# An encoder layer on one core: the merge gates in seven-product pairs, on inputs normalised in place

## The chip, the core and the metric

The kernel runs on one NeuronCore of a Trainium2 chip. The metric is device time in microseconds, from several executions; one further execution is recorded by the hardware profiler. Engines are named as in the profile: PE is TensorE (PEld its weight loads), DVE is VectorE, ACT is ScalarE, POOL is GpSimd, SP is SyncE, which issues most of the DMAs.

## What is computed

One pre-norm residual layer over 256 tokens of width 2048, then a final RMSNorm. Everything is float32. Cut to what matters:

```
h    = rms_norm(x, norm_g)                              # (256, 2048)
proj = h @ w_in                                         # q k v o za | gif | xb zb | ga gb
ya   = mlstm(q, k, v, gif) * sigmoid(o) * silu(za)      # bidirectional, 4 heads of 512
yb   = rglru(xb) * silu(zb)                             # bidirectional recurrence, 2048 channels
merged = sigmoid(ga) * (ya @ w_branch_a) + sigmoid(gb) * (yb @ w_branch_b)
out  = rms_norm(x + merged @ w_out, final_g)
```

The work is matrix products of a 256 x 2048 input with weights of 2048 columns each: GA and GB are the two merge gates' products with h, and wa, wb, wo stand for w_branch_a, w_branch_b and w_out.

## The kernel before

**Products in three parts.** Each float32 operand is split in two float32r parts, hi and lo, and a product is the sum of three matmuls: hi·hi, hi·lo and lo·hi. A weight chunk (128 x 1024, 512 KB, for two of the 16 k-tiles of 128 and 512 output columns) is loaded by SP into one of five `raw` buffers; ScalarE casts it to `whi` (L123), VectorE subtracts to get `wlo` (L124). There are four buffers of each, so that a cast waits until TensorE has used the chunk four before it. `load_chunk` is that helper. A block is 512 output columns; it takes eight chunks (kq = 0 to 7) and has its sums in one `acc` tile (two of PSUM's eight banks, two such tiles). The other four banks are `aux` 0 to 3.

**Three forms of block.** `block_nat` gives a block with tokens on the partitions: per chunk 2 k-tiles x 2 token blocks x 3 = 12 matmuls of 512 columns (L138 to L140). `half_tr` gives the transposed form. `pair` takes two neighbouring blocks at once, and for the chunks in a given list it computes the 4 x 4 block products of two k-tiles, two token blocks and two column blocks with seven products in place of eight (a Winograd form). p1, p5, p7, p6 collect the common products, `banks` the rest. For such a chunk pair VectorE and ScalarE make sums of the weights (`t1`, `t2`) and split three of them, h1, h2, h3, and one half `b` (lines L157 and L158, buffers `b11`, `whi`, `wlo`), and `make_form` makes the sums of the inputs beforehand. Other chunks of a pair are plain, as in `block_nat`. After the last seven-product chunk the p's are combined into the result (L220 to L224), and after the last chunk the banks are added (L231).

**The order of the work.** q and k blocks, then four times a block of xb (`rg_block`) and a head (`head`: blocks V, O, Z and the head's output), then four zb blocks, the wb pairs, GB, GA and wa pairs interleaved, and wo: block 2, a pair of blocks 0 and 1, block 3 last. `h` is stored as hi and lo of x times norm_g, without the inverse root of the mean square, in the tile `sHL` (`hhi`, `hlo`); the factor per token is applied later, as `rstd` where tokens are on the partitions (a scale in the eviction), as the row `rbc` where they are on the free axis (a multiplication by VectorE). Small pieces of work (norms, gates, scores, the transposes `fin` and `fin_m`) stand in `queue` and `queue2` and are taken one at a time by `tick()`, once a chunk. Each engine's final order is set by a scheduler, by priorities in which `urgent()` work goes first in the order of the program, and by its own estimate of when operands are there.

Of the kernel before, what the change touches and what calls it, by code (L numbers as in the profile page):

```python
# [15 lines left out]
P = 128  # L16
S = 256
# [9 lines left out]
S_WB, S_WA, S_WO = (0, 2, 4), (0, 2), (0, 2)  # L27
# [10 lines left out]
def hybrid_encoder(ctx: ExitStack, tc: tile.TileContext, x, xt, pk, bif, fg, wg, wi, wr, wa, wb, wo, out):  # L38
# [104 lines left out]
    def pair(src, xhi, xlo, forms, dst, b11):  # L143
        accs = [acc_pair()[0] for _ in range(2)]
        p1, p5, p7, p6 = accs[0] + accs[1]
        banks = [None] * 4
        began = set()
        d11, d12, d21, d22 = dst
# [14 lines left out]
        def products(kq, last):  # L163
# [28 lines left out]
            if banks[0] is None:  # L192
                banks[:3] = [aux(i) for i in range(3)]
# [4 lines left out]
            mm(banks[2], *xb(1, 1), h2[:, rt_], l2[:, rt_], False)  # L198
            mm(banks[0], *xb(1, 0), h3[:, rt_], l3[:, rt_], False)
            mm(banks[1], *sf(3), h3[:, lf], l3[:, lf], False)  # L200

        def plain(kq, jj, last):
            hi, lo = load_chunk(src[jj][kq])
            if banks[3] is None:
                banks[3] = aux(3)
            for kk in range(KC):
                o = (kq * KC + kk) * S
                c = slice(kk * NB, (kk + 1) * NB)
                for tb in range(2):
                    mm(banks[tb * 2 + jj], xhi(o + tb * P, o + tb * P + P), xlo(o + tb * P, o + tb * P + P),  # L210
                       hi[:, c], lo[:, c], last and kk == KC - 1)

        final = max(forms)
        for kq in range(KT // KC):
            tick()
            if kq in forms:
                products(kq, kq == final)
                if kq == final:
                    with urgent():
                        act.copy(d11, p1)  # L220
                        dve.tensor_add(d12, p6, d11)
                        dve.tensor_add(d21, p7, d12)
                        dve.tensor_add(d12, p5, d12)
                        dve.tensor_add(d22, p5, d21)  # L224
            else:
                plain(kq, 0, kq == KT // KC - 1)
                tick()
                plain(kq, 1, kq == KT // KC - 1)
        with urgent():
            for i in (2, 0, 1, 3):  # L230
                dve.tensor_add(dst[i], dst[i], banks[i])  # L231
# [34 lines left out]
    def half_tr(src, half):  # L266
        ps, both = acc_pair()
        for kq in range(4):
# [6 lines left out]
            for k, m, o in tiles:  # L275
                pe.matmul(ps[m][:, :S], lo[:, o:o + P], hhi(k * S, (k + 1) * S),  # L276
                          start=False, stop=(k == KT - 1), skip_group_check=True)
# [126 lines left out]
    wt = sl("A")  # L404
# [3 lines left out]
    def wtv(dh, tb):  # L408
        return wt[:, (dh * 2 + tb) * S:(dh * 2 + tb + 1) * S]
# [20 lines left out]
    def r_row():  # L430
        ps = aux()
        pe.matmul(ps[:, :S], ones, diag, start=True, stop=True)
        dve.tensor_copy(rbc, ps[:, :S])

# [73 lines left out]
    def g_wts(h):  # L508
        for dh in (h, 4 + h):
# [4 lines left out]
            for tb in range(2):  # L514
# [11 lines left out]
              None, r_row, g_proj, None, g_nat, None, None, None, g_cum, g_rows, None, g_max]  # L526
# [82 lines left out]
    def rg_block(j):  # L609
        for i in range(2):  # L610
            both = half_tr(wi[BLK_XB + j], i)
# [3 lines left out]
            v = fold(None, both)  # L615
            with urgent():
                dve.tensor_mul(xp[:, 2 * i:2 * i + 2, 2:S + 2], v.rearrange("p (n s) -> p n s", n=2), rbc2)
# [82 lines left out]
    def head(h):  # L700
# [27 lines left out]
        def mix(tb):  # L728
# [14 lines left out]
            pool.tensor_mul(s_, s_, rstd[:, tb:tb + 1])  # L743
# [25 lines left out]
    ybh, ybl, ybf = [], [], {}  # L769

    def form_tiles(tag, kqs):
        t = sl(tag, F32R)
        return {kq: t[:, i * 1024:(i + 1) * 1024] for i, kq in enumerate(kqs)}

    for j in range(4):
        for i in range(2):
# [5 lines left out]
            v = zt[:, i * NB:(i + 1) * NB]  # L782
            fold(v, both)
            with urgent():
                v3 = v.rearrange("p (m s) -> p m s", m=2)
                dve.tensor_mul(v3, v3, rbc2)
# [7 lines left out]
        if j == 0:  # L794
            ybf = form_tiles("PT", S_WB)
        for kq in (2 * j, 2 * j + 1):
            if kq in ybf:
                make_form(None, ybf[kq], sg[:, (kq % 2) * NB:(kq % 2 + 1) * NB])
    ybh, ybl = Cols(ybh, 1024), Cols(ybl, 1024)
    yah, yal = Cols([yas["h"]], 4096), Cols([yas["l"]], 4096)  # L800

    def alternate(make):
        n = [0]

        def nxt():
            n[0] += 1
            return make(n[0] % 2)

        return nxt

    sgb = sl("E")
    for p in range(2):
        pair((wb[2 * p], wb[2 * p + 1]), ybh, ybl, ybf,
             [sgb[:, (4 * p + i) * NB:(4 * p + i + 1) * NB] for i in (0, 2, 1, 3)],
             alternate(lambda i: hp.tile([P, 2 * NB], F32R, tag=("to", "zz")[i], name=name("b11"))))
    yaf = form_tiles("PT", S_WA)
    for j in range(4):
        ps = block_nat(wi[BLK_GB + j], hhi, hlo)
        tg = hp.tile([P, 2 * NB], F32, tag="to" if j % 2 == 0 else "zz", name=name("gb"))
        with urgent():  # L820
            for tb in range(2):
                act.activation(tg[:, tb * NB:(tb + 1) * NB], ps[tb], AF.Sigmoid, scale=rstd[:, tb:tb + 1])
        v = sgb[:, j * 1024:(j + 1) * 1024]
        dve.tensor_mul(v, v, tg)
        if j == 0:
            for kq in yaf:
                make_form([t(kq * NB, (kq + 1) * NB) for t in (yah, yal)], yaf[kq])

    mht, mlt, mf_ = [], [], {}
    for p in range(2):  # L830
        tgs = []
        for j in (2 * p, 2 * p + 1):
            tg = hp.tile([P, 2 * NB], F32, tag="to" if j % 2 == 0 else "zz", name=name("tg"))
            tgs.append(tg)
            ps = block_nat(wi[BLK_GA + j], hhi, hlo)
            with urgent():
                for tb in range(2):
                    act.activation(tg[:, tb * NB:(tb + 1) * NB], ps[tb], AF.Sigmoid, scale=rstd[:, tb:tb + 1])
        tmp = [sl(f"C{i}", F32, 1024) for i in (2, 3)]
        dst = [tmp[jj][:, tb * NB:(tb + 1) * NB] for tb in range(2) for jj in range(2)]  # L840
# [150 lines left out]
```

## Time and profile before

| | us |
|---|---|
| median of 3 runs (lowest, highest) | 1039.34 (1037.99, 1041.29) |
| profiled execution | 1038.49 |
| its span | 1036.5 |
| PE busy, DVE busy, ACT busy in the span | 1025.0, 739.0, 567.5 |

The busy time of PE counts matmuls to their modelled ends, which overlap, so that 99% is not a measure of how densely they follow. The granted TensorE clock is 0.999 of full speed over the span. In rows of groups, the last columns are busy time and mean duration of one, then the idle time of the engine just before the group and what ended it. Timeline rows begin with start and duration in us from the span's start.

### The profile page before, as it was taken

The numbers are of one execution on the slowest core, as the hardware profiler recorded it, in microseconds if no ns is written. First come the engines' busy times: TensorE is split into PE (matmuls) and PEld (weight loads), VectorE is DVE, ScalarE is ACT, GpSimd is POOL, SyncE is SP. The second block draws the span as 40 slices with busy tenths as digits, with TensorE's granted clock in tenths as the row PEclk, the third lists the DMA queues.
The fourth block names the chain that finished last, engine by engine and source line by source line (L and its number), as shares of the span: only waits on it lengthen the run. The fifth ranks groups of instructions, "written<-read, shape, count | busy, mean of one in ns | idle before, by whom it ended". The sixth has DMA issues, their size and how long they took to land.

```text
span 1036.5 us, 13627 instructions
## 1 busy us (share of the span) xinstructions
PE 1025.0 (99%) x5142; PEld 870.9 (84%) x5142; DVE 739.0 (71%) x976; ACT 567.5 (55%) x750; POOL 12.6 (1%) x43
## 2 busy tenths in 40 slices
PE   9999999999999999999999999999999999999997
PEld 8988888888888888888888878888888888888886
DVE  6677785697579639854977899854555766768974
ACT  7545447756765684568455564534444534544552
POOL 1000000000000000000000000000000000000000
PEclk9999999999999999999999999999999999999999
DMA  9654445565556555555555456666566465577562
GB/s 351 249 181 143 163 163 183 172 196 180 177 191 192 180 177 191 188 190 168 197 185 190 149 192 211 213 201 200 182 196 202 175 212 175 192 254 263 184 202 82
DMA packets 55954, 199.32 MB, mean 192 GB/s; under 512 B 6352, under 2 KB 6864, under 8 KB 55504
## 3 DMA queue, kind: packets, MB, share of 16 engines
q1 hardware_dynamic: 55024, 197.13, 56.7%
q10 hardware_dynamic: 864, 1.32, 0.3%
q8 instruction: 40, 0.66, 0.3%
q14 instruction: 26, 0.21, 0.1%
HBM read 196.33 MB, written 2.10 MB: 191 GB/s over the span
## 4 chain that ended last, share of the span: by engine, by line
PE 96%; DVE 2%; DMA 1%; ACT 1%; issue 0%; SPq 0%; DVEq 0%; ACTq 0%
PE acc L273 16%; PE acc L138 15%; PE acc L139 15%; PE acc L140 15%; PE acc L276 8%; PE aux L154 5%; PE aux L153 5%; PE aux L151 5%; PE acc L151 1%; PE aux L736 1%; PE acc L153 1%; PE acc L154 1%; DMA raw<-wo 1%; PE aux L917 1%; PE aux L649 1%; PE aux L648 1%
## 5 line engine op out<-in xcount | busy, mean ns | idle before, releaser
L124 DVE TENSOR_TENSOR wlo<-raw,whi 128x1024 fp32r<-128x1024 f32 (+1 forms) x329 | 399.7, 1220 | 233.1 <-ACT whi L123 231.0
L123 ACT CAST whi<-raw 128x1024 fp32r<-128x1024 f32 (+1 forms) x329 | 342.7, 1049 | 331.0 <-PE acc L140 143.4
L138 PE MATMUL acc<-whi,sHL 128*128 128x512 f32 x640 | 250.1, 391 | 0.0
L139 PE MATMUL acc<-wlo,sHL 128*128 128x512 f32 x640 | 249.8, 390 | 0.0
L140 PE MATMUL acc<-whi,sHL 128*128 128x512 f32 x640 | 249.4, 390 | 0.0
L273 PE MATMUL acc<-sHL,whi 128*128 128x512 f32 x704 | 179.0, 395 | 0.0
L273 PEld LDWEIGHTS acc<-sHL,whi 128*128 128x128 f32 x704 | 127.0, 189 | 23.6
L140 PEld LDWEIGHTS acc<-whi,sHL 128*128 128x128 f32 x640 | 120.2, 188 | 25.1
L138 PEld LDWEIGHTS acc<-whi,sHL 128*128 128x128 f32 x640 | 120.3, 188 | 24.4
L139 PEld LDWEIGHTS acc<-wlo,sHL 128*128 128x128 f32 x640 | 120.3, 188 | 23.9
L276 PEld LDWEIGHTS acc<-sHL,wlo 128*128 128x128 f32 x704 | 96.1, 190 | 7.1
L276 PE MATMUL acc<-sHL,wlo 128*128 128x256 f32 x704 | 98.7, 283 | 0.0
L153 PE MATMUL aux<-wlo,sC 128*128 128x512 f32 x144 | 56.1, 390 | 0.0
L154 PE MATMUL aux<-whi,sD 128*128 128x512 f32 x144 | 56.1, 390 | 0.0
L151 PE MATMUL aux<-whi,sC 128*128 128x512 f32 x144 | 52.3, 390 | 1.2 <-ACT whi L157 1.2
L154 PE MATMUL aux<-whi,sB 128*128 128x512 f32 x104 | 40.5, 390 | 0.0
L153 PE MATMUL aux<-wlo,sA 128*128 128x512 f32 x104 | 40.5, 390 | 0.0
L157 ACT CAST whi<-t 128x1024 fp32r<-128x1024 f32 x24 | 25.0, 1052 | 24.3 <-DVE t L173 8.2
L151 PE MATMUL aux<-whi,sA 128*128 128x512 f32 x104 | 38.2, 390 | 0.0
L151 PEld LDWEIGHTS aux<-whi,sC 128*128 128x128 f32 x144 | 27.0, 188 | 7.1 <-ACT whi L157 1.6
L153 PEld LDWEIGHTS aux<-wlo,sC 128*128 128x128 f32 x144 | 27.0, 188 | 5.7
L154 PEld LDWEIGHTS aux<-whi,sD 128*128 128x128 f32 x144 | 27.0, 188 | 5.6
(319 smaller groups left out, 1195.3 us busy)
## 6 DMA issues: line engine op xcount, KB each, us to landing
raw<-wi SPq DMA_DIRECT2D x255, 512.0 KB, 4.0
raw<-wb SPq DMA_DIRECT2D x32, 512.0 KB, 3.9
raw<-wa SPq DMA_DIRECT2D x32, 512.0 KB, 3.6
raw<-wo SPq DMA_DIRECT2D x32, 512.0 KB, 4.5
raw<-wr SPq DMA_DIRECT2D x8, 512.0 KB, 3.7
sB<-x SPq DMA_DIRECT2D x4, 512.0 KB, 8.3
sA<-x SPq DMA_DIRECT2D x1, 2048.0 KB, 9.1
sA<-xt SPq DMA_DIRECT2D x7, 256.0 KB, 7.0
```

What stands on the lines that cost most here:

```text
L123: last_copy[0] = act.copy(hi[:, r], raw[:, r]).ins
L124: last_sub[0] = dve.tensor_sub(lo[:, r], raw[:, r], f(hi[:, r])).ins
L138: pe.matmul(ps[tb], a, wh, start=(k == 0), stop=False)
L139: pe.matmul(ps[tb], a, wl, start=False, stop=False)
L140: pe.matmul(ps[tb], b, wh, start=False, stop=(k == KT - 1))
L151: pe.matmul(ps, a, wh, start=id(ps) not in began, stop=False)
L153: pe.matmul(ps, a, wl, start=False, stop=False)
L154: pe.matmul(ps, b, wh, start=False, stop=stop)
L157: act.copy(hi, v)
L273: pe.matmul(ps[m], hi[:, o:o + P], hl_t[:, 2 * k * S:2 * (k + 1) * S], start=(k == 0), stop=False, skip_group_check=True)
L276: pe.matmul(ps[m][:, :S], lo[:, o:o + P], hhi(k * S, (k + 1) * S), start=False, stop=(k == KT - 1), skip_group_check=True)
L648: pe.matmul(dst, whi[:, o:o + P], xl[:, r], start=False, stop=False)
```

## The change

The lists of seven-product chunks are now given for each pair and are kq 0 and 4 in every one: wb goes from three chunks (0, 2, 4) to two, wa and wo keep two, and GB and GA, which were eight single blocks, become four pairs with two each. Inside `pair`, p1 to p6 lie in the four `aux` banks and the plain sums in both `acc` tiles, one tile for each block. The chunks up to the last seven-product one are done for both blocks; then the p's are combined; then the rest of the first block is done, its sum added (L230) and its epilogue done, and then the same for the second block. The order of GB, GA and wa is now both GB pairs, both GA pairs, both wa pairs.

So that a pair's result needs no factor per token, h is normalised in place. When `rbc` is there, `x_scale` makes x times norm_g times `rbc` in the slot B (16 multiplications of 256 columns). While the second half of the first xb block reads `sHL` for the last time, `h_renew` writes the normalised hi and lo over it, four k-tiles after each chunk. All later scales by `rstd` and all later multiplications by `rbc` go. The merged values go to the slot of `sHL`, and of wo's last block only the first four chunks have slots of their own (all eight had).

```
-S_WB, S_WA, S_WO = (0, 2, 4), (0, 2), (0, 2)
+S_WB, S_GB, S_GA, S_WA = [((0, 4), (0, 4))] * 4
+S_WO = (0, 4)
...
-    def pair(src, xhi, xlo, forms, dst, b11):
-        accs = [acc_pair()[0] for _ in range(2)]
-        p1, p5, p7, p6 = accs[0] + accs[1]
-        banks = [None] * 4
+    def pair(src, xhi, xlo, forms, kqs, dst, b11, epilogue):
+        aps = [aux(i) for i in range(4)]
+        p1, p5, p7, p6 = aps
+        accs = [acc_pair()[1] for _ in range(2)]
+        banks = [[v[:, :NB], v[:, NB:]] for v in accs]
...
+        last = max(kqs)
+        for kq in range(last + 1):
+            if kq in kqs:
+                products(kq, kq == last)
             else:
-                plain(kq, 0, kq == KT // KC - 1)
+                plain(kq, 0)
+                plain(kq, 1)
+        with urgent():
+            act.copy(d11, p1)
+            dve.tensor_add(d12, p6, d11)
+            dve.tensor_add(d21, p7, d12)
+            dve.tensor_add(d12, p5, d12)
+            dve.tensor_add(d22, p5, d21)
+        for jj in range(2):
+            for kq in range(last + 1, kl + 1):
                 tick()
-                plain(kq, 1, kq == KT // KC - 1)
-        with urgent():
-            for i in (2, 0, 1, 3):
-                dve.tensor_add(dst[i], dst[i], banks[i])
...
+                plain(kq, jj)
+            with urgent():
+                dve.tensor_add(dst[jj], dst[jj], accs[jj])
+                epilogue(jj)
...
+    def x_scale(i):
+        if i == 0:
+            hn.append(sl("B"))
+        for k in range(4 * i, 4 * i + 4):
+            r = slice(k * S, (k + 1) * S)
+            dve.scalar_tensor_tensor(out=hn[0][:, r], in0=xs[:, r], scalar=ng_[:, k:k + 1], in1=rbc,
+                                     op0=ALU.mult, op1=ALU.mult)
+
+    def h_renew(i):
+        h4 = hl_t[:, i * 8 * S:(i + 1) * 8 * S].rearrange("p (k q s) -> p k q s", q=2, s=S)
+        v = hn[0][:, i * 4 * S:(i + 1) * 4 * S].rearrange("p (k s) -> p k s", s=S)
+        with urgent():
+            act.copy(h4[:, :, 0, :], v)
+            dve.tensor_sub(h4[:, :, 1, :], v, f(h4[:, :, 0, :]))
...
-              None, r_row, g_proj, None, g_nat, None, None, None, g_cum, g_rows, None, g_max]
+              None, r_row, g_proj, lambda: x_scale(0), g_nat, lambda: x_scale(1), lambda: x_scale(2),
+              lambda: x_scale(3), g_cum, g_rows, None, g_max]
...
-            both = half_tr(wi[BLK_XB + j], i)
+            both = half_tr(wi[BLK_XB + j], i, h_renew if j == 0 and i == 1 else None)
...
-            with urgent():
-                dve.tensor_mul(xp[:, 2 * i:2 * i + 2, 2:S + 2], v.rearrange("p (n s) -> p n s", n=2), rbc2)
+            v = xp[:, 2 * i:2 * i + 2, 2:S + 2]
+            fold(v, both)
+            if j == 0:
+                with urgent():
+                    dve.tensor_mul(v, v, rbc2)
...
     for p in range(2):
-        tgs = []
-        for j in (2 * p, 2 * p + 1):
-            tg = hp.tile([P, 2 * NB], F32, tag="to" if j % 2 == 0 else "zz", name=name("tg"))
-            tgs.append(tg)
-            ps = block_nat(wi[BLK_GA + j], hhi, hlo)
-            with urgent():
...
+        gb = [sl(f"D{2 * p + i}", F32, 1024) for i in range(2)]
+
+        def epi_gb(jj, p=p, gb=gb):
+            act.activation(gb[jj], gb[jj], AF.Sigmoid)
+            dve.tensor_mul(sgv[2 * p + jj], sgv[2 * p + jj], gb[jj])
+
+        pair((wi[BLK_GB + 2 * p], wi[BLK_GB + 2 * p + 1]), hhi, hlo, forms("h"), S_GB[p], gb, b11, epi_gb)
+    ga = []
+    for p in range(2):
+        ga += [sl(f"C{2 * p + i}", F32, 1024) for i in range(2)]
+
+        def epi_ga(jj, p=p):
+            act.activation(ga[2 * p + jj], ga[2 * p + jj], AF.Sigmoid)
+
+        pair((wi[BLK_GA + 2 * p], wi[BLK_GA + 2 * p + 1]), hhi, hlo, forms("h"), S_GA[p], ga[2 * p:], b11, epi_ga)
...
+        def epi_wa(jj, p=p, wd=wd):
+            j = 2 * p + jj
+            dve.tensor_mul(ga[j], ga[j], wd[jj])
+            dve.tensor_add(ga[j], ga[j], sgv[j])
...
+        pair((wa[2 * p], wa[2 * p + 1]), yah, yal, forms("a"), S_WA[p], wd, b11, epi_wa)
...
     for kq in range(8):
-        o = (kq % 4) * KC * NB
-        ch.append(load_chunk(wo[3][kq], dst=[lw[(kq // 4) * 2 + i][:, o:o + KC * NB] for i in range(2)]))
+        if kq < 4:
+            ch.append(load_chunk(wo[3][kq], dst=[sl(f"C{kq}", F32R, 1024), lw[:, kq * 1024:(kq + 1) * 1024]]))
+        else:
+            ch.append(load_chunk(wo[3][kq]))
```

The lines of the changed kernel that the order of its instructions names: L124 and L125 are the cast and subtraction of a plain chunk, L160 and L161 those of a seven-product chunk, L175 to L181 its sums, L230 the add after a block, L455 and L456 the cast and subtraction of `h_renew`, L596 to L609 the heads' scores, L649 to L656 the convolution, L821 to L827 zb's gate, L855 GB's gate product.

More of the change, by code (lines that the diff above doesn't have):

```diff
@@ L197, in products, with plain @@
             mm(p6, *sf(1), h2[:, lf], l2[:, lf], last)
[L198 to L202, printed above, removed]
+            mm(banks[0][1], *xb(1, 1), h2[:, rt_], l2[:, rt_], False)
+            mm(banks[0][0], *xb(1, 0), h3[:, rt_], l3[:, rt_], False)
+            mm(banks[1][0], *sf(3), h3[:, lf], l3[:, lf], False)
+        def plain(kq, jj):
             hi, lo = load_chunk(src[jj][kq])
-            if banks[3] is None:
-                banks[3] = aux(3)
             for kk in range(KC):
@@ L264, in block_first, with half_tr @@
         return ps
-    def half_tr(src, half):
+    def half_tr(src, half, after=None):
         ps, both = acc_pair()
@@ L408, in wtv @@
     def wtv(dh, tb):
-        return wt[:, (dh * 2 + tb) * S:(dh * 2 + tb + 1) * S]
+        if not wt_:
+            wt_.append(sl("A"))
+        return wt_[0][:, (dh * 2 + tb) * S:(dh * 2 + tb + 1) * S]
     diag = et([P, S])
@@ L767, in hybrid_encoder, with form, h_form, ya_form @@
     hs = rg["hs"]
[L769 to L773, printed above, removed]
+    ybh, ybl = [], []
+    fslot = {}
+    fm_t = []
+    def form(x, kq, i, **kw):
+        fslot[x, kq] = fm_t[0][:, i * 1024:(i + 1) * 1024]
+        make_form(fslot[x, kq], **kw)
+    def h_form(kq, i):
+        h4 = hl_t[:, kq * 4 * S:(kq + 1) * 4 * S].rearrange("p (k q s) -> p k q s", q=2, s=S)
+        form("h", kq, i, parts=[h4[:, :, q, :] for q in range(2)])
+    def ya_form(kq, i):
+        form("a", kq, i, parts=[t(kq * NB, (kq + 1) * NB) for t in (yah, yal)])
+    def forms(x):
+        return {kq: v for (n, kq), v in fslot.items() if n == x}
+    k_yb, k_h, k_ya = (sorted(set(sum(v, ()))) for v in (S_WB, S_GB + S_GA, S_WA))
     for j in range(4):
@@ L781, in hybrid_encoder @@
                 sg = hp.tile([P, 2 * NB], F32, tag="to", name=name("sg"))
[L782 to L786, printed above, removed]
+            fold(zt[:, i * NB:(i + 1) * NB], both)
         act.activation(sg, zt, AF.Sigmoid)
@@ L811, in hybrid_encoder, with b11 @@
+    def b11():
+        nb11[0] += 1
+        return hp.tile([P, 2 * NB], F32R, tag=("to", "zz")[nb11[0] % 2], name=name("b11"))
     sgb = sl("E")
+    sgv = [sgb[:, j * 1024:(j + 1) * 1024] for j in range(4)]
     for p in range(2):
[L813 to L827, printed above, removed]
```

153 lines of the change are left out of this document (68 added, 85 removed).

## The prediction

> **What bounds the kernel now.** I read the page's busy line and its chain first, to see which engine sets the end; then the list of TensorE's waits, to see how much of that engine's time is not work; then the timeline at the places that the change touches, and the stage windows there.
>
> ```profile
> PE 1025.0 (99%) x5142; PEld 870.9 (84%) x5142; DVE 739.0 (71%) x976; ACT 567.5 (55%) x750; POOL 12.6 (1%) x43
> PE 96%; DVE 2%; DMA 1%; ACT 1%; issue 0%; SPq 0%; DVEq 0%; ACTq 0%
> PE aux L151 <- ACT whi L157: 1.2, 1, 1.2
> PE aux L301 <- DVE wu L333: 1.1, 1, 1.1
> PE acc L263 <- DVE wlo L124: 0.8, 1, 0.8
> PE acc L151 <- ACT b L157: 0.6, 1, 0.6
> PE aux L917 <- DVE yd L231: 0.4, 1, 0.4
> ```
>
> TensorE is 96% of the chain that ended last, and its whole list of waits is five, 4.1 us by modelled ends. So the time is the number of matmuls times their spacing, plus those few waits. A change gains by fewer matmuls or by a wait removed; it loses only if it makes TensorE wait anew. Here is the spacing, read from two lo parts that VectorE makes in a plain stage (one chunk each, started when TensorE frees a slot):
>
> ```profile
> 686.52 1.23 DVE L124 TENSOR_TENSOR wlo<-raw,whi 128x1024 fp32r<-128x1024 f32 x1 [1.50 <-ACT whi L123]
> 689.24 1.23 DVE L124 TENSOR_TENSOR wlo<-raw,whi 128x1024 fp32r<-128x1024 f32 x1 [1.49 <-ACT whi L123]
> ```
>
> 2.72 us for a chunk's 12 matmuls of 512 columns: 0.227 us each. The 390 ns that the page gives for one is its latency, not its rate. The Trainium skill (TensorE: Matmul & The Clock Gate, Back-to-back issue gap) puts the sustained spacing at N=512 at about 131 ns. By it the saving below would be an estimated 18 x 0.131 = 2.4 us; these rows say 0.227, and they decide.
>
> **The matmuls removed.** A seven-product chunk pair costs 7 x 3 = 21 matmuls, a plain one 2 blocks x 2 x 2 x 3 = 24. Before, 6 + 4 + 2 = 12 chunk pairs (wb, wa, wo) are done in sevens. Now 4 each in wb, GB, GA and wa, and 2 in wo: 18. That is 6 more x 3 = 18 matmuls fewer, all 512 wide: 18 x 0.227 = **4.1 us**, all on the path. So the forms can't be the whole story of a larger gain; the rest must come from waits.
>
> **The wait at the entry of the wb pairs.** Spacing above 0.23 is lost time, also where the list shows less because it counts from modelled ends:
>
> ```profile
> 601.71 0.39 PE L154 MATMUL aux<-whi,sD 128*128 128x512 f32 x1
> 603.27 0.50 PE L151 MATMUL aux<-whi,sC 128*128 128x512 f32 x1 [1.18 <-ACT whi L157]
> 604.41 0.50 PE L151 MATMUL acc<-b,sC 128*128 128x512 f32 x1 [0.63 <-ACT b L157]
> 604.74 0.39 PE L151 MATMUL acc<-whi,sPT 128*128 128x512 f32 x1
> ```
>
> 1.56 - 0.23 = 1.33 us, then 1.14 - 0.23 = 0.91: 2.2 us. Both wait for ScalarE. Its queue there, before (`whi_1161`, `1164`, `1166` belong to the second seven-product chunk, `b11_1135` to the first):
>
> ```order
> L284 COPY fold_1124_5443<-acc_1107_5354 128x512
> L123 CAST whi_1154_5526<-raw_1153_5525 128x1024
> L787 ACTIVATE sg_1103_5349<-zt_1102_5348 128x1024
> L157 CAST whi_1161_5553<-t1_1160_5550 128x1024
> L157 CAST whi_1164_5560<-t2_1163_5557 128x1024
> L157 CAST b11_1135_5461<-raw_1133_5457 128x512
> L792 CAST sC3_1127_5450<-sg_1103_5349 128x1024
> ```
>
> and now, from the same fold on:
>
> ```order
> L288 COPY fold_1116_5448<-acc_1099_5359 128x512
> L124 CAST whi_1145_5530<-raw_1144_5529 128x1024
> L821 ACTIVATE sg_1096_5355<-zt_1095_5354 128x1024
> L124 CAST whi_1149_5548<-raw_1148_5547 128x1024
> L124 CAST whi_1153_5566<-raw_1152_5565 128x1024
> L124 CAST whi_1157_5584<-raw_1156_5583 128x1024
> L160 CAST b11_1130_5469<-raw_1128_5465 128x512
> L826 CAST sC3_1118_5454<-sg_1096_5355 128x1024
> ```
>
> Three casts of the second seven-product chunk have left, since that chunk is now kq=4 and not 2, and plain casts with no VectorE work ahead of them took their place. On TensorE the first product with `b11` stood 34 matmuls after zb's last one and now stands 58 after it: 24 x 0.227 = 5.4 us later, more than the 0.91 that it was late. The second chunk's `t2` part was used after 33 matmuls and now after more than 96. I take the whole 2.2 us as gained; bounds 0 (something else is late instead) and 2.2.
>
> **The wait at the end of the wo pair.**
>
> ```profile
> 1005.73 0.39 PE L154 MATMUL aux<-whi,sD 128*128 128x512 f32 x1
> 1006.51 0.39 PE L917 MATMUL aux<-sHL,sC 128*128 128x256 f32 x1 [0.39 <-DVE yd L231]
> ```
>
> 0.78 - 0.23 = 0.55 us: wo's last block needs an `aux` bank that the pair's last add (L231) still reads. Now the `aux` banks hold p1, p5, p7, p6, emptied six plain chunks (16 us) before. Gained: 0.55, bound 0.
>
> **What VectorE gets in return.** Its instructions, from these rows:
>
> ```profile
> L124 DVE TENSOR_TENSOR wlo<-raw,whi 128x1024 fp32r<-128x1024 f32 x327 | 398.4, 1223 | 233.1 <-ACT whi L123 231.0
> L123 ACT CAST whi<-raw 128x1024 fp32r<-128x1024 f32 x327 | 341.6, 1051 | 331.0 <-PE acc L140 143.4 <-PE acc L273 69.7 <-PE aux L154 63.7
> L231 DVE TENSOR_TENSOR sE<-sE,aux 128x512 f32<-128x512 f32 x8 | 5.2, 682 | 0.0
> L172 DVE TENSOR_TENSOR t<-raw 128x512 f32<-128x512 f32 x12 | 8.3, 688 | 5.6 <-DMA raw<-wa 3.9 <-DMA raw<-wb 1.6
> L321 DVE SCALAR_TENSOR_TENSOR sHL<-sA,ngain,sHL 128x256 fp32r<-128x256 f32 x16 | 7.0, 481 | 3.7 <-ACT sHL L320 3.7
> L617 DVE TENSOR_TENSOR xp<-fold,rbc 128x512 f32<-128x512 f32 x8 | 5.5, 692 | 0.2
> 40.00:50.00 10.00, 10.00 (x66) 8.93 (x65) 6.89 (x10) 4.26 (x5) 0.00 (x0) 1.00 0.69 212
> 126.00:142.00 16.00, 16.00 (x94) 14.08 (x93) 15.70 (x49) 5.91 (x8) 0.00 (x0) 1.00 0.48 161
> 639.00:685.00 46.00, 46.00 (x204) 38.12 (x203) 40.40 (x52) 23.53 (x25) 0.00 (x0) 1.00 0.64 215
> ```
>
> A seven-product chunk costs it 5 x 0.69 + 3 x 1.22 = 7.1 us against TensorE's 21 x 0.227 = 4.8; a plain chunk 1.22 against 2.72. A pair now (2 sevens, 12 plain, 4 combining adds of 0.69, two adds from PSUM of some 2 x 0.68 each, two gate products of 1.22) takes it about 37 us of TensorE's 2 x 4.8 + 12 x 2.72 = 42, 88%. Before, a wb pair with three sevens filled 40.40 of 46 us (88%) in the last window above and TensorE did not wait in it. So the pairs fit, with the same margin and better spread: sevens four chunks apart, not two. ScalarE is at half load in the same row (23.53 of 46).
>
> *x_scale*: 16 x 0.48 = 7.7 us, in bursts of nine and seven, as soon as the row `rbc` is there (45.6). VectorE was 69% busy from 40 to 50. The lo part that stands behind both bursts had this slack:
>
> ```profile
> 45.18 0.42 DVE L433 COPY rbc<-aux 128x256 f32<-128x256 f32 x1
> ...
> 49.51 1.23 DVE L124 TENSOR_TENSOR wlo<-raw,whi 128x1024 fp32r<-128x1024 f32 x1 [1.21 <-ACT whi L123]
> 59.80 1.11 PE L276 MATMUL acc<-sHL,wlo 128*128 128x256 f32 x8
> ```
>
> It was done at 50.7 and first used at 59.8: 9 us against at most 7.7. Cost 0.
>
> *h_renew*: 4 x 1.05 us on ScalarE (a cast of 1024 columns took 1051 ns) and 4 x 1.22 = 4.9 on VectorE, between 128 and 142, where VectorE is 98% busy (15.70 of 16). This is the tightest place. The queue of VectorE before, from the lo part of head 0's first V chunk to that of the second:
>
> ```order
> L124 TENSOR_TENSOR wlo_297_1537<-raw_295_1535,whi_296_1536 128x1024
> L577 TENSOR_TENSOR rd_255_1359<-rd_255_1359,em_178 128x4
> L626 SCALAR_TENSOR_TENSOR sD0_283_1500<-xp_1230,pks_73,sD0_283_1500 128x256 x2
> L572 SCALAR_TENSOR_TENSOR sA_30_179,den_261_1402<-aux_260_1389,rq_148,sA_30_179 128x128
> L572 SCALAR_TENSOR_TENSOR sA_30_179,den_261_1402<-aux_260_1389,rq_148,sA_30_179 128x256 x2
> ```
>
> and now:
>
> ```order
> L125 TENSOR_TENSOR wlo_302_1562<-raw_300_1560,whi_301_1561 128x1024
> L601 TENSOR_TENSOR rd_256_1376<-rd_256_1376,em_178 128x4
> L652 SCALAR_TENSOR_TENSOR sD0_288_1525<-xp_1247,pks_73,sD0_288_1525 128x256 x2
> L456 TENSOR_TENSOR sHL_5_90<-sB_103_613,sHL_5_90 128x4x256
> L596 SCALAR_TENSOR_TENSOR sA_158_898,den_263_1421<-aux_262_1408,rq_148,sA_158_898 128x128
> L596 SCALAR_TENSOR_TENSOR sA_158_898,den_263_1421<-aux_262_1408,rq_148,sA_158_898 128x256 x2
> ```
>
> One L456 went in behind each of four lo parts; what it delays is score and convolution work (L596, L652) that nothing waits for yet. The lo parts had this lead:
>
> ```profile
> 128.85 1.22 DVE L124 TENSOR_TENSOR wlo<-raw,whi 128x1024 fp32r<-128x1024 f32 x1
> 138.29 0.40 PE L139 MATMUL acc<-wlo,sHL 128*128 128x512 f32 x1
> ```
>
> Done at 130.1, used at 138.3: 8.2 us against 4.9. Cost 0, upper bound 4.9. The multiplications by the inverse norm that go (14 x 0.69 = 9.7 us of VectorE, in xb's later blocks and zb, and eight one-column ones on GpSimd) lay beside matmuls: gain 0. Evictions of V, O, Z keep their length without the scale.
>
> **The hand-over of PSUM.** Each pair holds all four `aux` and both `acc` tiles. The next pair's first 18 matmuls need only `aux` and `acc` 0; the nineteenth needs `acc` 1, which is read by an add after the pair's very last matmul. Cover: 18 x 0.227 = 4.1 us, against the add's 1.3. VectorE's queue where GB's first pair hands over to the second (L230 is that add, `t1_1380` to `wlo_1387` the next pair's preparation):
>
> ```order
> L230 TENSOR_TENSOR sD0_1285_6117<-sD0_1285_6117,acc_1291_6123 128x1024
> L181 TENSOR_TENSOR t2_1383_6466<-raw_1378_6453,t2_1383_6466 128x512
> L161 TENSOR_TENSOR wlo_1382_6463<-t1_1380_6459,whi_1381_6462 128x1024
> L855 TENSOR_TENSOR sE_1120_5458<-sE_1120_5458,sD0_1285_6117 128x1024
> L161 TENSOR_TENSOR wlo_1385_6470<-t2_1383_6466,whi_1384_6469 128x1024
> L161 TENSOR_TENSOR wlo_1387_6474<-raw_1378_6453,whi_1386_6473 128x1024
> L230 TENSOR_TENSOR sD1_1286_6118<-sD1_1286_6118,acc_1292_6124 128x1024
> ```
>
> where before plain chunks ran through with one product per block:
>
> ```order
> L124 TENSOR_TENSOR wlo_1344_6308<-raw_1342_6306,whi_1343_6307 128x1024
> L124 TENSOR_TENSOR wlo_1348_6326<-raw_1346_6324,whi_1347_6325 128x1024
> L824 TENSOR_TENSOR sE_1129_5454<-sE_1129_5454,gb_1332_6267 128x1024
> L124 TENSOR_TENSOR wlo_1352_6344<-raw_1350_6342,whi_1351_6343 128x1024
> L124 TENSOR_TENSOR wlo_1356_6362<-raw_1354_6360,whi_1355_6361 128x1024
> L124 TENSOR_TENSOR wlo_1360_6380<-raw_1358_6378,whi_1359_6379 128x1024
> ```
>
> The add stands right behind the next pair's last lo part, whose slot comes free one chunk before the pair ends, so I cost it 0. **wo's last block** now has own slots for four chunks only; the last slot comes free with the pair's end and its chunk is first used 42 matmuls (9.5 us) later, against 1.05 + 1.22 us of preparation: 0.
>
> **The sum**: 4.1 + 2.2 + 0.55 = 6.9 us less. The profiled execution took 1038.49 (span 1036.5), so 1031.6; the median of the runs is 0.85 higher, 1039.34, so **1032.4**.
>
> **Rivals.** (1) *One wait moves*: the entry wait, or one of its size, turns up at another pair's start, VectorE still being slower than TensorE through a seven-product chunk (7.1 against 4.8). Then 4.1 + 0.55 remain, 1034.7. Against it: the wb pair that ran without a wait. (2) *The renewal is not absorbed*: the 98% window passes its 4.9 us on to TensorE, 6.9 - 4.9 = 2.0 left, 1037.3, no measurable change. Against it: 8.2 us of lead. (3) *Slower, by the hand-over*: if the add comes behind a whole preparation (7.1 us), it ends 7.1 + 1.3 - 4.1 = 4.3 us too late at each of the seven boundaries between the eight pairs, 30 us, 1062. It decides from 6.9 / 7 = 1.0 us a boundary on. For it: one more queue entry between last matmul and next pair than before; against it: the order above. (4) *The clock*: if short idles at bank changes halved the granted clock for those 4.1 us at each boundary, 7 x 4.1 = 29 us would be added to 1032, 1061. The clock read 1.00 through the window from 639 to 685, which holds a pair change. The Trainium skill (same page, A second HAM failure mode: psum-queue depth-cycling) describes just that for a kernel that cycles PSUM banks; this trace shows none of it. That the change does not do what it says is out: TensorE's order has 3722 matmuls of 512 columns where 3740 were.
>
> **Chances.** Forecast 0.64, (1) 0.19, (2) 0.08, (3) 0.07, (4) 0.02. Faster than by 0.3% (3.1 us, about what this measurement can tell) are the first two, 0.83; within it (2), 0.08; slower (3) and (4), 0.09. The range holds the first two cases: from 1030.6 (the lowest run, 1037.99, less 6.9 is 1031.1; 0.5 below that for runs lower than the three shown) to 1036.2 (case 1 at 1034.7 and 1.5 for one more small wait or a run at the upper end).
>
> **What would show it.** 5124 matmuls in the busy line; L151's and L917's waits gone from TensorE's list; its last matmul 6.9 us earlier; VectorE about 50 us busier (28 more instructions of 1024 columns, 21 of 512 and 16 of 256, 8 of 512 fewer: 34 + 14 + 8 - 6) with TensorE unmoved at 128 to 142. A wait of TensorE for L230, L456 or L161 would prove me wrong, and name which rival.

## The result and the profile after

The changed kernel takes 1030.69 us (median of 4 runs, 1030.13 to 1031.18); the kernel before took 1039.51 in the same session (4 runs, 1037.99 to 1041.29). The ratio is 0.9914, 95% interval 0.9897 to 0.9932: 8.9 us less on 1039.3, between 7.1 and 10.7. The forecast was 6.9 us less, 1032.4. The direction and the list of terms came out; the size was 2 us short. Taken off the 1039.34 that the forecast set out from, 8.9 us give 1030.4, just under the lower end of its range, 1030.6. The rest of this document is about those 2 us. The later sessions have 64 more timed runs of the kernel before, with a mean of 1039.3, and one of them has five more of the changed kernel, with a mean of 1030.8: 8.5 us apart, so that the shortfall is between 1.3 us (by the medians of that session, 8.2) and 2 us.

The busy line, the chain and the whole list of TensorE's waits of the changed kernel (columns of a wait: us in total, times, longest):

```profile
PE 1019.5 (99%) x5124; PEld 867.3 (84%) x5124; DVE 786.2 (76%) x1039; ACT 580.1 (56%) x763; POOL 11.3 (1%) x35
PE 98%; DMA 1%; DVE 0%; SPq 0%; ACT 0%; issue 0%; DVEq 0%
PE aux L305 <- DVE wu L337: 1.1, 1, 1.1
PE acc L265 <- DVE wlo L125: 0.8, 1, 0.8
```

5124 matmuls, as counted. Both waits that are left lie in the first 11 us; the two on L151 and the one on L917 are gone, and VectorE has 47 us more to do (786.2 against 739.0; 50 were forecast) without TensorE waiting for it. The timeline of TensorE at the three places that the sum spoke of, the entry of the wb pairs, the hand-over from the last wb pair to the first GB pair with VectorE's last add between them, and the end of the wo pair:

```profile
601.73 0.39 PE L157 MATMUL acc<-whi,sD 128*128 128x512 f32 x1
601.95 0.39 PE L154 MATMUL acc<-whi,sC 128*128 128x512 f32 x1
...
678.11 0.39 PE L157 MATMUL acc<-whi,sD 128*128 128x512 f32 x1
678.54 1.22 DVE L230 TENSOR_TENSOR sE<-sE,acc 128x1024 f32<-128x1024 f32 x1 [0.36 <-PE acc L157]
682.42 0.39 PE L154 MATMUL acc<-whi,sPT 128*128 128x512 f32 x1
...
998.78 0.39 PE L157 MATMUL acc<-whi,sHL 128*128 128x512 f32 x1
999.01 0.39 PE L950 MATMUL aux<-sB,sHL 128*128 128x512 f32 x1
```

The entry and the end run at 0.23 us a matmul. At the hand-over the pair's last matmul starts at 678.11, the add runs from 678.54 to 679.76, and the next pair first needs that bank at 682.42: 2.7 us to spare. From the first matmul of the GB pairs to the first of the wa pairs that goes to an `acc` tile TensorE issues 789 matmuls in 178.84 us, 0.2267 each, so nothing is lost in the four new pairs.

The spans are 1036.5 and 1028.6 us, 7.9 apart, 1.0 more than forecast; 0.70 of that lies in the first 50 us. The medians are 8.8 apart because the profiled execution of before was, by chance, one of the shorter ones: 1.0 us under its median, that of the changed kernel 0.3 under its own.

### The profile page after: what moved, and what is told of

It reads as the page before. It is cut to its first block, busy times and chain, and to the rows that moved or that the text cites. A ratio compares the mean times of both kernels' runs of the same rounds, so it can differ in the third digit from the quotient of the medians.

```text
span 1028.6 us, 13664 instructions
## 1 busy us (share of the span) xinstructions
PE 1019.5 (99%) x5124; PEld 867.3 (84%) x5124; DVE 786.2 (76%) x1039; ACT 580.1 (56%) x763; POOL 11.3 (1%) x35
## 4 chain that ended last, share of the span: by engine, by line
PE 98%; DMA 1%; DVE 0%; SPq 0%; ACT 0%; issue 0%; DVEq 0%
PE acc L275 16%; PE acc L157 11%; PE acc L154 11%; PE acc L156 11%; PE acc L139 9%; PE acc L140 9%; PE acc L141 9%; PE acc L278 8%; PE aux L154 2%; PE aux L157 2%; PE aux L156 2%; PE aux L761 1%; PE aux L675 1%; PE aux L674 1%; PE aux L673 1%; PE aux L951 1%
## 5 line engine op out<-in xcount | busy, mean ns | idle before, releaser
L125 DVE TENSOR_TENSOR wlo<-raw,whi 128x1024 fp32r<-128x1024 f32 (+1 forms) x321 | 389.3, 1219 | 154.6 <-ACT whi L124 152.6
L124 ACT CAST whi<-raw 128x1024 fp32r<-128x1024 f32 (+1 forms) x321 | 334.4, 1048 | 267.7 <-PE acc L141 80.9
L139 PE MATMUL acc<-whi,sHL 128*128 128x512 f32 x416 | 162.4, 390 | 0.0
L140 PE MATMUL acc<-wlo,sHL 128*128 128x512 f32 x416 | 162.2, 390 | 0.0
L141 PE MATMUL acc<-whi,sHL 128*128 128x512 f32 x416 | 162.0, 389 | 0.0
L156 PE MATMUL acc<-wlo,sHL 128*128 128x512 f32 x260 | 101.1, 389 | 0.0
L157 PE MATMUL acc<-whi,sHL 128*128 128x512 f32 x260 | 101.1, 389 | 0.0
L154 PE MATMUL acc<-whi,sHL 128*128 128x512 f32 x260 | 99.5, 389 | 0.0
L141 PEld LDWEIGHTS acc<-whi,sHL 128*128 128x128 f32 x416 | 78.1, 188 | 16.3
L139 PEld LDWEIGHTS acc<-whi,sHL 128*128 128x128 f32 x416 | 78.2, 188 | 15.6
L140 PEld LDWEIGHTS acc<-wlo,sHL 128*128 128x128 f32 x416 | 78.2, 188 | 15.3
L160 ACT CAST whi<-t 128x1024 fp32r<-128x1024 f32 x36 | 37.9, 1053 | 57.4 <-PE acc L157 41.2
L157 PEld LDWEIGHTS acc<-whi,sHL 128*128 128x128 f32 x260 | 48.8, 188 | 10.2
L156 PEld LDWEIGHTS acc<-wlo,sHL 128*128 128x128 f32 x260 | 48.8, 188 | 10.2
L154 PEld LDWEIGHTS acc<-whi,sHL 128*128 128x128 f32 x260 | 48.8, 188 | 10.1
L161 DVE TENSOR_TENSOR wlo<-t,whi 128x1024 fp32r<-128x1024 f32 x36 | 44.0, 1223 | 14.6 <-ACT whi L160 14.6
L156 PE MATMUL acc<-wlo,sA 128*128 128x512 f32 x104 | 40.6, 390 | 0.0
L157 PE MATMUL acc<-whi,sB 128*128 128x512 f32 x104 | 40.5, 390 | 0.0
```

The source lines that it names most:

```text
L124: last_copy[0] = act.copy(hi[:, r], raw[:, r]).ins
L125: last_sub[0] = dve.tensor_sub(lo[:, r], raw[:, r], f(hi[:, r])).ins
L139: pe.matmul(ps[tb], a, wh, start=(k == 0), stop=False)
L140: pe.matmul(ps[tb], a, wl, start=False, stop=False)
L141: pe.matmul(ps[tb], b, wh, start=False, stop=(k == KT - 1))
L154: pe.matmul(ps, a, wh, start=id(ps) not in began, stop=False)
```

## The experiments

### The same two kernels again

No edit. First the kernel before against itself, then the changed one in five rounds, then a third trace of the kernel before.

> The kernel before, unchanged, timed against itself and profiled a second time. In the first pair of traces 0.70 us of the 7.84 us between the last matmuls lies in the first 50 us (4.94 us of spacing above normal there instead of 5.64), where I forecast nothing. If that is the arrival of the first loads and not the change, this trace shows a value between about 4.7 and 5.9 us there, other than 5.64, and a ratio of 1.000 within 0.002. If the change itself did it, it shows 5.6 again. The entry waits of the wb pairs (2.2 us) and the wait at the end of the wo pair (0.55 us) stand in both theories.

> The changed kernel again, five rounds. Theory 1 (the sum of 6.9 us is right but for small pieces, and the rest of the measured 8.8 us is the spread of four runs): a saving of 7.0 to 8.0 us, ratio 0.9925. Theory 2 (a term of 2 us was overlooked): 8.8 us again, ratio 0.9915.

> The kernel before once more, for a third trace. By the clock's theory its stretch from 601 to 609 us shows one of the two pictures seen: 2.2 to 2.4 us above normal spacing at a granted clock of 1.00, or about 4.5 us with a stretch of 3.4 us at 0.50. A value between, at full clock, speaks against it.

Measured: before against before 1039.69 to 1039.13, ratio 1.0004 (0.9993 to 1.0015); after 1030.93, ratio 0.9921 (0.9908 to 0.9934), 8.2 us, between what the two theories gave. What decided was a place that I had not asked about, the entry of the wb pairs. The stage windows at the entry of the first wb pair (600 to 610 us) and of the second (640 to 660); the second column of PE is the number of matmuls, then come the other engines, the granted clock, the DMA share and GB/s. First the profiled execution of before that the prediction was made from, then its second and its third trace, then the changed kernel:

```profile
600.00:610.00 10.00, 8.19 (x36) 6.22 (x35) 9.16 (x11) 6.56 (x9) 0.00 (x0) 1.00 0.34 112
640.00:660.00 20.00, 20.00 (x90) 16.58 (x89) 17.95 (x25) 10.01 (x10) 0.00 (x0) 1.00 0.60 211
```

```profile
600.00:610.00 10.00, 8.20 (x28) 6.04 (x27) 8.51 (x10) 4.98 (x7) 0.00 (x0) 0.83 0.30 100
640.00:660.00 20.00, 19.77 (x86) 15.72 (x85) 18.41 (x23) 10.36 (x11) 0.00 (x0) 1.00 0.52 178
```

```profile
600.00:610.00 10.00, 8.20 (x35) 6.22 (x35) 9.16 (x11) 6.57 (x9) 0.00 (x0) 1.00 0.30 107
640.00:660.00 20.00, 19.35 (x82) 14.82 (x82) 18.24 (x23) 9.76 (x11) 0.00 (x0) 1.00 0.53 175
```

```profile
600.00:610.00 10.00, 10.00 (x46) 8.28 (x45) 9.57 (x11) 6.13 (x7) 0.00 (x0) 1.00 0.76 269
640.00:660.00 20.00, 20.00 (x90) 16.53 (x89) 16.60 (x23) 10.19 (x12) 0.00 (x0) 1.00 0.58 207
```

Against the changed kernel's 46 and 90 matmuls, the three executions of before are short of 10 and 0, of 18 and 4, of 11 and 8. At 0.227 us each that is 2.3, 5.0 and 4.3 us (2.4, 4.8 and 4.1 by the spacing of the matmuls in these windows, which no edge of a window cuts). So the forecast's 2.2 us was read correctly from the cheapest of three executions.

The second trace at the first entry shows how 2.2 becomes 4.1 (TensorE's rows, then windows of 1 us):

```profile
602.83 0.50 PE L151 MATMUL aux<-whi,sC 128*128 128x512 f32 x1 [1.18 <-ACT whi L157]
603.96 0.50 PE L151 MATMUL acc<-b,sC 128*128 128x512 f32 x1 [0.62 <-ACT b L157]
...
605.01 0.63 PE L151 MATMUL acc<-whi,sPT 128*128 128x512 f32 x1
605.44 0.63 PE L153 MATMUL acc<-wlo,sPT 128*128 128x512 f32 x1
```

```profile
604.00:605.00 1.00, 1.00 (x4) 0.81 (x5) 1.00 (x3) 0.86 (x1) 0.00 (x0) 0.95 0.00 0
605.00:606.00 1.00, 1.00 (x4) 0.79 (x3) 1.00 (x1) 0.00 (x0) 0.00 (x0) 0.50 0.03 8
606.00:607.00 1.00, 1.00 (x4) 0.81 (x3) 0.12 (x1) 0.47 (x1) 0.00 (x0) 0.50 0.89 238
607.00:608.00 1.00, 1.00 (x3) 0.72 (x3) 0.39 (x1) 1.00 (x2) 0.00 (x0) 0.50 0.68 279
608.00:610.00 2.00, 2.00 (x9) 1.65 (x8) 2.00 (x3) 0.82 (x2) 0.00 (x0) 0.92 0.14 20
```

The waits of 1.18 and 0.62 are the same as before. But 2.1 us after the first one ends the granted clock falls to 0.50, from about 604.9 to 608.3, 3.4 us, and the matmuls come 0.43 us apart instead of 0.23: some eight of them, 0.20 us each, 1.6 us lost, which no list of waits shows. In the other two traces the clock stays at 1.00 through the same two waits.

The traces show what makes the difference. In all fourteen of this case the granted clock changes only at whole multiples of 3.413 us after its first rise; in the second trace it rises at 4.16, falls at 604.90, which is 176 of these steps later, and rises again at 608.32, one step on. Cut along this grid, the second trace has both waits in one step, 601.49 to 604.90: TensorE stands 2.3 us of it by spacing. In the first trace an edge at 603.80 parts them, 1.6 us and 0.7; in the third an edge at 603.50, 1.3 and 1.0. The Trainium skill (TensorE: Matmul & The Clock Gate, What's actually happening) says that the clock is halved after an idle window, that the window is 3.413 us long, and that it runs freely and not from the kernel's start; the grid agrees with the length and with the free run. The same page's advice (Why this matters for your kernels) is to avoid idle gaps of over about 3 us; here two gaps of 1.3 and 0.9 us by spacing were enough, and the measurement decides.

The timed runs fit: of the 64 of the kernel before, the 11 with a mean clock of 0.996 average 1040.8 us and the 16 with 0.999 average 1038.3; none of the nine of the changed kernel is below 0.998.

The third trace shows the first trace's picture at the entry, 2.4 us at full clock. It pays in another way, at the start of the second wb pair:

```profile
643.57 0.40 PE L151 MATMUL aux<-whi,sC 128*128 128x512 f32 x1
644.21 0.50 PE L151 MATMUL aux<-whi,sPT 128*128 128x512 f32 x1 [0.24 <-DVE sE L231]
...
645.01 0.62 PE L151 MATMUL aux<-whi,sC 128*128 128x512 f32 x2
645.94 0.50 PE L153 MATMUL aux<-wlo,sC 128*128 128x512 f32 x1 [0.31 <-DVE wlo L124]
```

Here TensorE waits for the add of the pair before (L231) and then for a lo part. In the first trace that start ran without a wait, and I took it as proof that three sevens in a wb pair fit; in the second and third it lost 0.8 and 1.7 us by spacing.

The first 50 us hold another spread: summed start-to-start distance above normal 5.64, 5.19 and 5.80 us in the three traces of before, 4.94 and 5.69 in two of after. It differs between executions of one kernel by as much as between the kernels, so the 0.70 us that the first pair of traces differs by there is not the change's.

### The entry wait alone, in the kernel before

```
-S_WB, S_WA, S_WO = (0, 2, 4), (0, 2), (0, 2)
+S_WB, S_WA, S_WO = (0, 4), (0, 2), (0, 2)
```

> The kernel before with one edit: its wb pairs take seven products in chunks 0 and 4 instead of 0, 2 and 4; 6 matmuls more (1.4 us). Two theories of the entry wait's price. My prediction's: it costs the 2.2 us that the profiled execution shows, so this kernel's last matmul comes 2.2 - 1.4 = 0.8 us earlier and the time falls by 0.8 us. The rival after the second look at before: in about half of the executions the wait also drops the granted clock to 0.5 for 3.4 us, 2.2 us more each time, so the mean falls by about 0.8 + 1.1 = 1.9 us, and the runs lie closer together (before: 1037.0 to 1043.1 in 49 runs; here within about 2 us). If the wait has another cause than the chunk so close behind, it stays, the clock too, and the time rises by 1.4 us.

Measured: 1037.29 us (11 runs, 1036.51 to 1039.08) against 1039.35, ratio 0.9982 (0.9973 to 0.9991): 2.1 us faster with 6 matmuls, 1.4 us, more. So the starts of the wb pairs cost 3.4 us in timed runs (2.06 + 1.36; 2.3 to 4.2 by the interval), not 2.2. The windows and ScalarE's row for `b11`, and then ScalarE's two rows of the kernel before for which TensorE waited:

```profile
600.00:610.00 10.00, 10.00 (x46) 8.29 (x45) 10.00 (x12) 6.21 (x7) 0.00 (x0) 1.00 0.75 251
640.00:660.00 20.00, 20.00 (x90) 16.58 (x89) 14.72 (x20) 9.95 (x11) 0.00 (x0) 1.00 0.57 204
600.63 0.62 ACT L157 CAST b<-raw 128x512 fp32r<-128x512 f32 x1 [0.92 <-DVE sg L789]
```

```profile
602.18 1.04 ACT L157 CAST whi<-t 128x1024 fp32r<-128x1024 f32 x1 [1.66 <-PE aux L154]
603.74 0.62 ACT L157 CAST b<-raw 128x512 fp32r<-128x512 f32 x1 [0.51 <-DVE sg L789]
```

46 and 90 matmuls: no wait at either start. `b11`'s cast comes at 600.6 where it came at 603.7. So the chunk close behind did cause the wait, as my step said, but not by casts in ScalarE's queue: ScalarE stood idle ahead of both casts. `b11` takes the buffer of zb's `zt`, whose last reader is VectorE's L789; before, that started at 602.48, behind a sum and a lo part of the second chunk, and here it starts at 599.37. The other cast stood 1.66 us for one of the four `whi` buffers, which TensorE's last matmul ahead of the wait released. The rival theory, that the wait's price is larger than the one execution showed, gave 1.9 us and fits; the forecast's 0.8 lies outside the interval (0.9 to 2.8), if barely.

### The chunk close behind, put back into the changed kernel

```
-S_WB, S_GB, S_GA, S_WA = [((0, 4), (0, 4))] * 4
+S_WB = ((0, 2), (0, 2))
+S_GB, S_GA, S_WA = [((0, 4), (0, 4))] * 3
```

> The changed kernel with the two seven-product chunks of each wb pair at chunks 0 and 2 instead of 0 and 4; the count of matmuls is the same. If the entry wait of before came from the second seven-product chunk standing so close that its preparation is queued ahead of other casts (my step), 0.9 to 2.2 us of waiting on ScalarE come back in front of the first pair, and the time is that much above the changed kernel. If the wait went for another reason (a pair now begins with the aux banks already free), no wait and the same time within 0.3 us in the trace.

Measured: 1030.66 us, ratio 0.9921 (0.9908 to 0.9933), the same as the changed kernel (1030.93): no wait. ScalarE's queue, and the first product with `b11` on TensorE:

```profile
597.56 1.03 ACT L161 CAST whi<-t 128x1024 fp32r<-128x1024 f32 x1
601.86 1.05 ACT L161 CAST whi<-t 128x1024 fp32r<-128x1024 f32 x1 [3.27 <-DVE t L182]
602.82 1.05 ACT L161 CAST whi<-raw 128x1024 fp32r<-128x1024 f32 x1
603.77 0.61 ACT L161 CAST b<-raw 128x512 fp32r<-128x512 f32 x1
...
606.78 0.39 PE L155 MATMUL aux<-b,sC 128*128 128x512 f32 x1
```

All three casts of the second chunk stand ahead of `b11` here (in the kernel before, two did), and `b11` is as late as in the kernel before (604.4). Yet TensorE asks for it only at 606.8: with p5, p7, p6 in `aux` and the plain chunks in `acc` it has 22 matmuls, 5.0 us, more to do first. So the chunk close behind is not enough for the wait; it also takes the early place of `b11`'s product.

### The banks of before in the changed kernel

```
-        aps = [aux(i) for i in range(4)]
-        p1, p5, p7, p6 = aps
-        accs = [acc_pair()[1] for _ in range(2)]
-        banks = [[v[:, :NB], v[:, NB:]] for v in accs]
+        aps = [acc_pair()[0] for _ in range(2)]
+        p1, p5, p7, p6 = aps[0] + aps[1]
+        banks = [[aux(2 * j + i) for i in range(2)] for j in range(2)]
```

(and the last add of a block is made for each bank by itself)

> The changed kernel with the banks of before: in every pair p1, p5, p7, p6 lie in the two acc tiles again and the plain chunks in the four aux banks; the number of matmuls and the chunks in sevens (0 and 4) stay. The order now puts the first product with b11 35 matmuls behind zb's last one, as before, and not 58. Theory A (my step: the wait at the entry went because the casts of a second seven-product chunk no longer stand ahead of b11's): no wait there, and only the wait at the end of the wo pair, about 0.5 us, comes back. Theory B (the exchange of banks removed it, because p5, p7, p6 and the plain chunks can start before b11 is there): b11's high part, ready about 9.1 us after zb's last matmul in the changed kernel's trace, is wanted after 35 x 0.227 = 7.9 us, so about 1 us of waiting comes back there, beside the 0.5 us.

Measured: 1036.1 us, ratio 0.9973 (0.9962 to 0.9984), 5.2 us over the changed kernel. Theory B failed at the entry: no wait there either. Together with the run before: in the changed kernel each of the two, the later place of `b11`'s product and the second chunk two places further back, keeps the entry wait away. The 5.2 us lie somewhere that neither theory named:

```profile
PE aux L880 <- DVE sC L888: 2.3, 1, 2.3
PE acc L139 <- ACT sHL L296: 1.1, 1, 1.1
935.16 0.40 PE L140 MATMUL acc<-wlo,sHL 128*128 128x512 f32 x1
937.90 2.75 PE L880 MATMUL aux<-ident,sC 128*128 128x128 f32 x12 [2.34 <-DVE sC L888]
940.88 0.63 PE L139 MATMUL acc<-whi,sHL 128*128 128x512 f32 x1
```

After the last wa pair the transposes (L880) need `aux` banks and the finished gates. With the plain chunks in `aux`, these banks and both blocks' adds come free only at the pair's end; with them in `acc`, `aux` is empty in the middle of a pair (read from the code and these rows, not tested by itself). TensorE stands 1.1 and 2.3 us (1.3 and 2.5 by spacing), and here too the clock goes to 0.50 for 3.4 us behind it; in the ten timed runs its mean was 0.995 to 0.997 (0.998 or 0.999 in the changed kernel), so this happens in nearly all of them. The wait at the end of the wo pair, which both theories expected, did not come back, so the exchange of banks is not shown to be what removed it.

### Fewer sevens: the price of a matmul

```
-S_WB, S_GB, S_GA, S_WA = [((0, 4), (0, 4))] * 4
+S_WB = S_WA = ((0, 4), (0, 4))
+S_GB = S_GA = ((0,), (0,))
```

> The changed kernel with one seven-product chunk in each merge-gate pair (GB and GA) instead of two: 4 chunk pairs back to plain, 12 matmuls of 512 columns more. By the spacing of 0.227 us it takes 2.7 us more than the changed kernel. If the seven-product chunks cost TensorE waits that no list shows, it takes less than that; if a matmul of a seven-product chunk costs 0.131 us, 1.6 us.

Measured: 1032.95 us, ratio 0.9946 (0.9934 to 0.9958), 2.0 us over the changed kernel by medians and 2.5 by means (runs from 1032.86 to 1034.03), against 2.7 expected. In the traces the gates' stretch is 3.2 us longer with 14 matmuls more between its ends (803 in 182.01 us, 0.2267 each; two of the 14 are a matter of order at the ends): 0.227, and not 0.131. The timed runs alone, 2.0 and 2.5 between 1.6 and 2.7, would not have told the two apart.

### The renewal written twice

```
             act.copy(h4[:, :, 0, :], v)
             dve.tensor_sub(h4[:, :, 1, :], v, f(h4[:, :, 0, :]))
+            act.copy(h4[:, :, 0, :], v)
+            dve.tensor_sub(h4[:, :, 1, :], v, f(h4[:, :, 0, :]))
```

> The changed kernel with the renewal of the normalised input written twice, the same values both times: four more copies of 1024 columns on ScalarE and four more subtractions on VectorE (4 x 1.13 us start to start = 4.5 us) between 128 and 142 us. By my step the lo parts behind it have lead: in the changed kernel's trace the shortest lead there is 4.3 us, so 4.5 us more costs 0 to 0.5 us. By the rival (the window is full, nothing is absorbed) TensorE stands 4.5 us longer and the time is 4.5 us above the changed kernel.

Measured: 1030.99 us, ratio 0.9924 (0.9912 to 0.9935), the same as the changed kernel within 0.1 us; no wait in the list. The windows of this kernel:

```profile
126.00:142.00 16.00, 15.96 (x92) 13.71 (x91) 16.00 (x38) 12.50 (x15) 0.00 (x0) 1.00 0.37 128
142.00:160.00 18.00, 18.00 (x90) 15.10 (x89) 18.00 (x30) 11.85 (x17) 0.00 (x0) 1.00 0.52 174
```

VectorE is busy without a break for 34 us and TensorE goes on: the shortest lead of a lo part made between 126 and 155 us falls from 4.3 us to 0.1, so this was just what the window could still take. A VectorE at 100% is no proof of a cost; the lead of what it makes is.

### More sevens

All three are edits of the same lists of the changed kernel.

```
A: S_WB, S_GB, S_GA, S_WA = [((0, 2, 4), (0, 2, 4))] * 4;  S_WO = (0, 2, 4)
B: the same with (0, 3, 5)
C: S_WB = S_GA = ((0, 2, 4), (0, 2, 4));  S_GB = S_WA = ((0, 4), (0, 2, 4));  S_WO = (0, 4)
D: as the changed kernel, but S_GB = ((0, 4), (0, 2, 4)), S_GA = ((0, 2, 4), (0, 2, 4))
```

A:

> The changed kernel with three seven-product chunks (0, 2, 4) in every pair, wo's too: 27 chunk pairs instead of 18, 27 matmuls fewer. If the price is the matmul count alone, 27 x 0.227 = 6.1 us less than the changed kernel, about 1024.8. If VectorE becomes the bound (three such chunks in a row with one plain chunk pair between them: about 8.8 us of it against 10.2 us of TensorE by start-to-start distances, and a lead of 2.2 us to begin with), waits for lo parts appear at the starts of pairs and eat 1 to 6 us of it.

B:

> As the one before, with the three seven-product chunks at 0, 3 and 5: the same count of matmuls. If VectorE's bursts matter, fewer waits than with 0, 2, 4 where two plain chunk pairs follow the first seven, but the combining adds come later, with two chunks of each block left (4 x 2.7 = 10.9 us) before the next pair needs the banks; by the count alone again 6.1 us less than the changed kernel.

C:

> The changed kernel with three seven-product chunks (0, 2, 4) in both wb pairs, the second GB pair, both GA pairs and the second wa pair, two in the others: 24 chunk pairs instead of 18, 18 matmuls fewer. In the trace with three everywhere, the waits stood at the first GB pair (4.2 us), the first wa pair (1.2) and the wo pair (4.3) alone. If those come from the forms that VectorE must make just there, and are gone with two chunks in those pairs, the time is 18 x 0.227 = 4.1 us below the changed kernel, 1026.7. If VectorE's total work is the bound, the waits move on to the next pairs and no more than 2 us is gained.

D:

> The same with less: three seven-product chunks in the second GB pair and both GA pairs only: 21 chunk pairs instead of 18, 9 matmuls fewer, 9 x 0.227 = 2.0 us below the changed kernel, 1028.8, if no wait comes; the leads in those pairs of the trace with three everywhere went down to 0.07 to 0.8 us, so a wait of up to 1 us may come in some executions.

Measured: A 1035.44 us (0.9965, 0.9953 to 0.9977), B 1045.33 (1.0064, 1.0052 to 1.0076), C 1027.92 (0.9890, 0.9875 to 0.9905), D 1028.75 (0.9899, 0.9886 to 0.9913). Against the changed kernel's 1030.93, which was timed in an earlier session, three everywhere loses 4.5 us for 27 matmuls fewer, and B, where I hoped for less waiting, loses 14. TensorE's list in A, its window at the first GB pair and that of the wb pair ahead of it, and last the window of B at its first GB pair:

```profile
PE aux L154 <- ACT whi L160: 2.5, 3, 1.0
PE aux L156 <- DVE wlo L161: 1.1, 2, 0.9
PE acc L154 <- DVE sC L230: 0.6, 1, 0.6
676.00:686.00 10.00, 7.38 (x29) 4.83 (x28) 9.93 (x13) 5.99 (x6) 0.00 (x0) 1.00 0.20 58
640.00:676.00 36.00, 36.00 (x160) 29.64 (x159) 31.49 (x46) 18.06 (x21) 0.00 (x0) 1.00 0.60 200
677.00:688.00 11.00, 7.02 (x24) 4.91 (x23) 9.89 (x11) 5.30 (x6) 0.00 (x0) 0.84 0.21 71
```

In the wb pair VectorE keeps up (31.49 of 36 us, no wait); at the first GB pair it is full and late. One wait, on `acc` for L230, is the hand-over of my third rival: it exists, at 0.6 us once. B waits longer at the same places (its longest wait is 3.7 us), and its clock falls to 0.50 twice, for 3.4 us at the first GB pair and for 6.8 us at the wo pair, which in A's trace it never does. C takes the third seven away in the first GB pair, the first wa pair and wo alone, and the long waits go with it; one wait of 0.3 us is left at the first GB pair.

C is 3.0 us under the changed kernel for 18 matmuls fewer (4.1 us by the count), and D 2.2 for 9 (2.0). The waits followed the places and not VectorE's total. That the forms made at those places cause them was not tested by itself. C is the fastest version run, 1.1% under the kernel before.

## Where the prediction held, and the step that failed

**Matmuls, 4.1 us: right.** 18 fewer at 0.227; the new pairs run at 0.2267 through 178.84 us.

**The entry wait, 2.2 us, bounds 0 and 2.2: mis-sized, and this is the step that failed.** The spacing rows gave 2.2, and I set the upper bound to the same number, as if the one execution showed the whole price. The three traces show 2.3, 5.0 and 4.3 us, a mean of 3.9; removing it alone was worth 3.4 us in timed runs. What comes on top is a stretch of half clock behind the wait in the second trace, and a late start of the second pair in the second and third. That the wait goes held, and so did the two reasons given for it, of which either keeps it away; but what made `b11` late stood in VectorE's queue and not, as the step has it, in ScalarE's.

**The wait at the end of wo, 0.55 us: right in this trace,** but in the second and third trace of before it is not in the list. Its mean over the three is nearer 0.2. The reason given, which bank the last block needs, is not shown: with the banks of before the wait stayed away.

**The step from the trace to the median, 0.85 us carried over unchanged: wrong.** I took the median's distance from the profiled execution as something that the change would leave alone. Part of it was the price of the entry that this execution, by luck, did not pay; after the change the distance is 0.32 (1030.69 and 1030.37). With 4.1, 3.9 and 0.2 the sum is 8.2 us, against spans that differ by 8.4 on the mean (1036.5, 1037.8, 1037.8 and 1028.6, 1029.4): few executions, but the timed means are 8.5 apart.

**Costs set to nothing: held.** The renewal could be doubled for free; `x_scale` brought no wait (none is left between 11 us and the end); the hand-over has 2.7 us to spare; that the removed multiplications gave nothing follows from the sum and was not tested by itself.

**Rivals.** The first, a wait that moves to another pair, did not happen here; A shows it with three sevens. The third and fourth did not happen in the changed kernel. But the fourth's mechanism, a clock halved by short idles, was real: it stood in other executions of the kernel *before*, of which I had only one, where the clock read 1.00. As a cost of the waits that the change removes it would have raised the forecast.

## What to carry to other kernels

A wait read from one profiled execution has a price in that execution; when the timed runs spread over more than the trace explains, take a second trace of the same kernel before setting the upper bound at what the first one shows. A short stop of TensorE can cost most of its length again (1.6 us behind 2.2 here), by a stretch of half clock that stands in the clock column and in no list of waits. And a full engine is judged by the lead of its products over their first use, place by place: in A three sevens were free inside the wb pair and cost 3.8 us by spacing at the start of the first GB pair.

## What the runs showed of the hardware that I had not expected

Stops far shorter than 3 us add up. The granted clock fell to 0.50 four times between its first rise and a kernel's last matmul: behind gaps of 1.3 and 0.9 us by spacing in one of three traces of the kernel before, behind stops of 1.3 and 2.5 us with the banks of before, and twice in B. On the grid of 3.413 us that the clock's changes keep to in every trace, TensorE stood 2.3, 2.9, 3.3 and 2.6 us of the step ahead of these falls, and at most 1.9 us of any other step at full clock up to the last matmul, in all fourteen traces. So what decides is how the grid cuts the stops; from 1.9 to 2.3 us no trace has a case. At half clock the 512-column matmuls came 0.427 us apart against 0.227, a factor of 1.9.
